# Log-sum-exp over rows: the first load as eight transfers of every eighth partition instead of two transfers of all partitions

## The chip, the cores and the metric

The kernel runs on one core of a Trainium2 chip. The metric is the device time of one execution in microseconds (us); the runs of the kernel before took 161.5 us in the median of three (161.47 to 161.6).

## The reference

```python
x = np.random.randn(32, 512, 1024).astype(np.float32)

def reference(x):
    max_x = np.max(x, axis=-1, keepdims=True)
    return (max_x.squeeze(-1) + np.log(np.sum(np.exp(x - max_x), axis=-1))).astype(np.float32)
```

The input has 16,384 rows of 1,024 numbers, 67.11 MB. One number comes out per row.

## The kernel before

The rows are laid over 128 partitions. Each partition owns 128 rows of 1,024 float32 (4 KB each): 112 that lie one behind another in memory, and 16 of a second block. The kernel takes the exponential without subtracting the maximum, sums it and takes the logarithm; a small side calculation finds out whether any sum left the range in which this is safe, and only then a second, slower branch is run. With this input it is not.

The input comes in 18 loads (table `LOADS`), from 16 rows per partition at the start down to half a row at the end. All go into `ring`, a buffer of 48 rows per partition, so three loads of 16 rows fit without waiting. For each load, in this order:

- SP (SyncE) issues the transfer in `load()`, after a wait for whoever still used that part of the ring. The transfer adds 16 to the semaphore `landed[i]` when it is complete.
- ScalarE (ACT in the profile) waits for `landed[i]` and takes the exponential in place (line 235).
- VectorE (DVE) sums each row, by `reduce_sum` (line 246, "R"), or after GpSimd (POOL, line 240) has added the two halves of each row ("F", summed in line 177), or with a fused add of the halves (line 256, "T").

So SP's issue of load 3 waits for VectorE's sum of load 0, which had its place in the ring, and so on round the ring. The last row goes in two pieces through line 209. Two stores write the logarithms; the first waits for the last load but one.

Load 0 is special in two ways. It is issued as two transfers: first `FIRST` = 512 elements of each partition (half a row, 2 KB), then the other 15.5 rows. ScalarE waits for both, with `landed[0]` at 16 for each transfer. And both issues are moved to the head of the program by `start_early`, ahead of the barrier with which all engines begin; `first_loads` holds them. Behind that barrier stand ScalarE's load of the function table (line 127), VectorE's memsets of constants (lines 128 to 131), and SP's issues of all other loads.

A load with all 128 partitions has 128 runs of memory, one per partition. A run is one packet of the profile: 64 KB for a load of 16 rows, 2 KB and 62 KB for the two parts of load 0. Sixteen packets are under way at a time.

Of the kernel before, what the change touches and what calls it, by code (L numbers as in the profile page):

```python
# [16 lines left out]
B = 16  # L17
LATE = 119
AHEAD = 1
FIRST = 512  # L20

# [31 lines left out]
def kernel(  # L55
# [5 lines left out]
    nc = tc.nc  # L61
# [4 lines left out]
    P = nc.NUM_PARTITIONS  # L66
# [19 lines left out]
    def source(e0, size):  # L86
        assert e0 >= W * d or e0 + size <= W * d
        return x_rest[:, e0 - W * d : e0 - W * d + size] if e0 >= W * d else x_rows[:, e0 : e0 + size]
# [8 lines left out]
    def sbuf(name, cols, dtype=fp32, rows=P):  # L97
        return nc.alloc_sbuf_tensor(name, [rows, cols], dtype).ap()

    ring = sbuf("ring", RING * d)  # L100
# [15 lines left out]
    landed = [nc.alloc_semaphore(f"landed{i}") for i in range(len(loads))]  # L116
# [19 lines left out]
    def load(i, here, done_before, size):  # L136
        for a, b, who, at in users:
            if a < here + size and b > here:
                sp.wait(who, at)
        users[:] = [u for u in users if not (u[0] < here + size and u[1] > here)]  # L140
        parts = [(0, FIRST), (FIRST, size)] if i == 0 else [(0, size)]
        return [
            nc.sync.dma_start(
                out=ring[:, here + a : here + b], in_=source(done_before + a, b - a)
            ).then_inc(landed[i], 16)
            for a, b in parts
        ]

    def check_early():
# [36 lines left out]
    here = 0  # L186
    early_sum = 0
    done_before = 0
# [3 lines left out]
    for i, (size, ops) in enumerate(loads):  # L192
# [3 lines left out]
        if any(q < here + size and q + t * d > here for _, t, q, _ in folded):  # L196
            reduce_folded()
        dma = load(i, here, done_before, size)
        if i < AHEAD:
            first_loads.extend(x.ins for x in dma)  # L200
# [3 lines left out]
        for k, (how, s) in enumerate(ops):  # L204
            rows = ring[:, p : p + s * d].rearrange("p (c d) -> p c d", d=d)
            if how in "YZ":
# [3 lines left out]
                    out=last_exp[:, here - p : end - p], in_=ring[:, here:end], func=AF.Exp,  # L210
# [4 lines left out]
                here = end  # L215
# [5 lines left out]
            elif how == "A":  # L221
# [3 lines left out]
                    out=v, in_=v, func=AF.Exp, accum_out=sumexp[:, c : c + 1]  # L225
# [5 lines left out]
            else:  # L231
# [4 lines left out]
                here = upto  # L236
            if how == "F":
# [3 lines left out]
                    out=rows[:, :, 0:H], in0=rows[:, :, 0:H], in1=rows[:, :, H:d], op=ALU.add  # L241
                ))
                folded.append((c, s, p, at))
            elif how == "R":
                dve.wait(act, at)
                who = (dve, dve.did(nc.vector.reduce_sum(  # L246
                    out=sumexp[:, c : c + s], in_=rows, axis=AX.X
                )))
                users.append((p, p + s * d, *who))
            elif how == "T":  # L250
# [3 lines left out]
                for r in range(s):  # L254
                    lo = rows[:, r, 0:H]
                    who = (dve, dve.did(nc.vector.scalar_tensor_tensor(  # L256
                        out=lo, in0=lo, scalar=1.0, in1=rows[:, r, H:d],
# [13 lines left out]
            if c == LATE:  # L271
# [4 lines left out]
                    out=res[:, 0:W], in_=sumexp[:, 0:W], func=AF.Ln  # L276
# [14 lines left out]
        out=res[:, LAST:NC], in_=last_sum, func=AF.Ln, bias=sumexp[:, LAST:NC]  # L291
# [8 lines left out]
        out=clamped[:, LATE:NC], in0=sumexp[:, LATE:NC], scalar=LOW,  # L300
# [10 lines left out]
        out=over[:, 0:half], in0=last_piece[:, 0:half], scalar=CEILING,  # L311
# [16 lines left out]
    with nc.If(all_fine < 1):  # L328
# [5 lines left out]
        for c0 in range(0, NC, RING):  # L334
# [6 lines left out]
            for c1, c2 in ((c0, edge), (edge, c0 + s)):  # L341
                if c1 == c2:
                    continue
                nc.scalar.dma_start(
                    out=ring[:, (c1 - c0) * d : (c2 - c0) * d],
                    in_=source(c1 * d, (c2 - c1) * d),
# [4 lines left out]
                out=neg, in_=v, op=ALU.max, axis=AX.X, negate=True  # L351
# [3 lines left out]
                out=v, in0=v, in1=neg[:, :, None].to_broadcast([P, s, d])  # L355
# [5 lines left out]
                out=sumexp[:, c0 : c0 + s], in_=v, axis=AX.X  # L361
# [71 lines left out]
```

## Time and profile before

| | |
|---|---|
| time, median of 3 runs | 161.5 us |
| the profiled execution's own time | 161.57 us |
| its span in the profile | 160.2 us |
| ACT busy | 114.5 us (71% of the span) |
| DVE busy | 114.3 us (71%) |
| POOL busy | 37.3 us (23%) |
| PE busy | 2.2 us (1%) |
| read from the chip's memory | 67.11 MB |

The span starts with SP's first issue. The page lists busy times by engine, and the span in 40 slices of 4.0 us. "SPq" is SP's queue of transfer issues; its rows tell how long the issue takes, not the transfer. A row of the timeline reads: start, length, engine, line, operation, output and input with shapes, how many instructions were merged; in brackets how long the engine was idle before, and what ended that.

### The profile page before, as it was taken

What the parts mean: (1) busy time and instruction counts of PE and PEld (TensorE: products, weight loads), DVE (VectorE), ACT (ScalarE), POOL (GpSimd) and SP (SyncE); (2) the same over time, 40 slices, a digit from 0 to 9 for tenths busy, and PEclk for the clock granted to TensorE, in tenths of its full rate; (3) what the DMA queues carried; (4) which work ended last, traced back from release to release, by engine and by line L of the source; (5) the groups of instructions that cost most, each with busy time, mean ns of one, the idle gap of its engine ahead of it and who ended that gap; (6) DMA issues with size and microseconds to landing.
All of it is one profiled execution on the core that took longest, in us unless ns stands there. A gap on an engine that the chain in (4) does not pass through costs nothing.

```text
span 160.2 us, 221 instructions
## 1 busy us (share of the span) xinstructions
PE 2.2 (1%) x26; PEld 1.1 (1%) x26; DVE 114.3 (71%) x59; ACT 114.5 (71%) x31; POOL 37.3 (23%) x11
## 2 busy tenths in 40 slices
PE   0000000000000000000000000000000000000022
PEld 0000000000000000000000000000000000000011
DVE  0000000009999499994999859959999999999996
ACT  3000059980799708995099949992999989799996
POOL 0000000000000000000000994690004969891000
DMA  9996996996996996997999999999999999999992
GB/s 319 507 460 301 507 524 262 524 524 262 524 524 262 524 524 262 524 474 311 483 442 442 442 425 409 409 409 471 423 414 417 458 409 399 444 412 428 415 408 97
DMA packets 3025, 67.18 MB, mean 419 GB/s; under 512 B 592, under 2 KB 720, under 8 KB 1488
## 3 DMA queue, kind: packets, MB, share of 16 engines
q1 hardware_dynamic: 3024, 67.18, 97.8%
q14 instruction: 1, 0.01, 0.0%
HBM read 67.11 MB, written 0.07 MB: 419 GB/s over the span
## 4 chain that ended last, share of the span: by engine, by line
DMA 51%; ACT 28%; DVE 19%; issue 1%; PE 0%
DMA ring<-in_x_dram 51%; ACT ring L235 28%; DVE sumexp L246 16%; DVE sumexp L177 2%; DVE ring L256 1%; DVE over L310 0%; PE count L315 0%; ACT res L275 0%; DVE clamped L299 0%; DVE fine L317 0%; DVE sumexp L219 0%
## 5 line engine op out<-in xcount | busy, mean ns | idle before, releaser
L235 ACT ACTIVATE ring<-ring 128x16384 f32<-128x16384 f32 (+16 forms) x23 | 111.7, 4908 | 42.3 <-DMA ring<-in_x_dram 42.3
L246 DVE TENSOR_REDUCE sumexp<-ring 128x16 f32<-128x16384 f32 (+4 forms) x9 | 85.6, 9513 | 42.1 <-ACT ring L235 42.1
L240 POOL TENSOR_TENSOR ring<-ring 128x3072 f32<-128x3072 f32 (+3 forms) x7 | 37.1, 5315 | 107.2 <-ACT ring L235 107.2
L177 DVE TENSOR_REDUCE sumexp<-ring 128x6 f32<-128x3072 f32 (+3 forms) x7 | 18.4, 2659 | 0.0
L256 DVE SCALAR_TENSOR_TENSOR ring<-ring 128x512 f32<-128x512 f32 x15 | 9.6, 687 | 0.4 <-ACT ring L235 0.4
L127 ACT ACT_TABLE_LOAD x1 | 1.3, 1283 | 1.9 <-PEq L64 1.9
L162 PE MATMUL count<-far,bad 128*1 128x1 f32 x2 | 0.2, 164 | 153.0 <-DVE clamped L157 153.0
L166 PE MATMUL count<-sumexp,ones 128*1 128x1 f32 x18 | 1.6, 164 | 3.6 <-DVE ring L256 3.6
L128 DVE MEMSET ones<- 128x1 f32 x1 | 0.1, 59 | 2.0 <-PEq L64 2.0
L256 DVE DVE_READ_ACCUMULATOR ring<-ring 128x1 f32 x15 | 1.2, 82 | 0.0
L209 ACT ACTIVATE last_exp<-ring 128x544 f32<-128x544 f32 (+1 forms) x2 | 1.2, 588 | 0.0
L162 PEld LDWEIGHTS count<-far,bad 128*1 128x1 f32 x2 | 0.1, 82 | 153.0 <-DVE clamped L157 153.0
L166 PEld LDWEIGHTS count<-sumexp,ones 128*1 128x1 f32 x18 | 0.8, 81 | 4.4 <-DVE ring L256 4.4
L310 DVE SCALAR_TENSOR_TENSOR over<-ring 128x240 f32<-128x240 f32 x1 | 0.4, 404 | 0.0
L317 DVE TENSOR_SCALAR fine<-count 1x1 int32<-1x1 f32 x1 | 0.1, 147 | 0.3 <-PE count L315 0.3
L157 DVE SCALAR_TENSOR_TENSOR clamped<-clamped,sumexp 128x119 f32<-128x119 f32 x1 | 0.3, 283 | 0.0
L275 ACT ACTIVATE res<-sumexp 128x112 f32<-128x112 f32 x1 | 0.3, 279 | 0.0
L290 ACT ACTIVATE res<-last_sum,sumexp 128x1 f32<-128x1 f32 x1 | 0.3, 261 | 0.0
L209 ACT ACTIVATION_READ_ACCUMULATOR last_exp<-ring 128x1 f32 x2 | 0.3, 129 | 0.0
L152 DVE TENSOR_SCALAR clamped<-sumexp 128x119 f32<-128x119 f32 x1 | 0.2, 222 | 0.0
L288 ACT ACTIVATE res<-sumexp 128x15 f32<-128x15 f32 x1 | 0.2, 213 | 0.0
L299 DVE SCALAR_TENSOR_TENSOR clamped<-sumexp 128x9 f32<-128x9 f32 x1 | 0.2, 170 | 0.0
(17 smaller groups left out, 1.8 us busy)
## 6 DMA issues: line engine op xcount, KB each, us to landing
ring<-in_x_dram SPq DMA_DIRECT2D x1, 7936.0 KB, 21.3
ring<-in_x_dram SPq DMA_DIRECT2D x1, 6912.0 KB, 23.9
ring<-in_x_dram SPq DMA_DIRECT2D x1, 6400.0 KB, 19.7
ring<-in_x_dram SPq DMA_DIRECT2D x1, 4608.0 KB, 15.9
ring<-in_x_dram SPq DMA_DIRECT2D x1, 3584.0 KB, 24.0
ring<-in_x_dram SPq DMA_DIRECT2D x1, 3072.0 KB, 19.1
ring<-in_x_dram SPq DMA_DIRECT2D x1, 2288.0 KB, 24.2
ring<-in_x_dram SPq DMA_DIRECT2D x1, 1664.0 KB, 20.9
```

Source lines behind the costliest of these rows:

```text
L127: nc.scalar.preload_act_table_set("natural_log_exp_and_others")
L157: dve.did(nc.vector.scalar_tensor_tensor(out=clamped[:, 0:LATE], in0=clamped[:, 0:LATE], scalar=0.0, in1=sumexp[:, 0:LATE], op0=ALU.bypass ...
L162: pe.did(nc.tensor.matmul(count, lhsT=bad[:, 0:1], rhs=far, start=True, stop=False))
L166: return pe.did(nc.tensor.matmul(count, lhsT=ones, rhs=sumexp[:, c : c + 1], **kw))
L177: at = dve.did(nc.vector.reduce_sum(out=sumexp[:, c0 : c0 + s0], in_=halves, axis=AX.X))
L209: at = act.did(nc.scalar.activation(out=last_exp[:, here - p : end - p], in_=ring[:, here:end], func=AF.Exp, accum_out=first_sum if how == ...
L235: at = act.did(nc.scalar.activation(out=v, in_=v, func=AF.Exp))
L240: at = pool.did(nc.gpsimd.tensor_tensor(out=rows[:, :, 0:H], in0=rows[:, :, 0:H], in1=rows[:, :, H:d], op=ALU.add))
L246: who = (dve, dve.did(nc.vector.reduce_sum(out=sumexp[:, c : c + s], in_=rows, axis=AX.X)))
L256: who = (dve, dve.did(nc.vector.scalar_tensor_tensor(out=lo, in0=lo, scalar=1.0, in1=rows[:, r, H:d], op0=ALU.mult, op1=ALU.add, accum_out ...
L275: ln_early = act.did(nc.scalar.activation(out=res[:, 0:W], in_=sumexp[:, 0:W], func=AF.Ln))
L310: dve.did(nc.vector.scalar_tensor_tensor(out=over[:, 0:half], in0=last_piece[:, 0:half], scalar=CEILING, in1=last_piece[:, half : 2 * half ...
```

## The change

Load 0 is issued as eight transfers instead of two. Transfer k, of 0 to 7, has the partitions k, k+8, ..., k+120, 16 of them, and all 16 rows of each: 16 runs of 64 KB. All eight add to the same semaphore, and ScalarE waits for 8 x 16 = 128. All eight go ahead of the opening barrier. The other loads are as they were, one transfer of 128 partitions each.

```diff
-FIRST = 512
+GROUP = 8
...
-        parts = [(0, FIRST), (FIRST, size)] if i == 0 else [(0, size)]
+        to, what = ring[:, here : here + size], source(done_before, size)
+        step = GROUP if i == 0 else 1
         return [
-            nc.sync.dma_start(
-                out=ring[:, here + a : here + b], in_=source(done_before + a, b - a)
-            ).then_inc(landed[i], 16)
-            for a, b in parts
+            nc.sync.dma_start(out=to[k:P:step], in_=what[k:P:step]).then_inc(landed[i], 16)
+            for k in range(step)
         ]
```

On SP, at the head of the program, there stood before (`in_x_dram` is the input; the branch in row 2 leaves the opening barrier; "dve" is VectorE's counter of finished instructions):

```order
0 L143 DMA ring<-in_x_dram 128x512
1 L143 DMA ring<-in_x_dram 128x15872
2 L428 UNCONDITIONAL_BRANCH [waits barrier_Pool_Activation_PE_DVE_SP_release]
3 L143 DMA ring<-in_x_dram 128x16384 [waits barrier_Pool_Activation_PE_DVE_SP_release]
4 L143 DMA ring<-in_x_dram 128x16384
5 L143 DMA ring<-in_x_dram 128x16384 [waits dve]
6 L143 DMA ring<-in_x_dram 128x13824 [waits dve]
```

And now:

```order
0 L144 DMA ring<-in_x_dram 16x16384 x8
1 L427 UNCONDITIONAL_BRANCH [waits barrier_Pool_Activation_PE_DVE_SP_release]
2 L144 DMA ring<-in_x_dram 128x16384 [waits barrier_Pool_Activation_PE_DVE_SP_release]
3 L144 DMA ring<-in_x_dram 128x16384
4 L144 DMA ring<-in_x_dram 128x16384 [waits dve]
5 L144 DMA ring<-in_x_dram 128x13824 [waits dve]
```

The two issues at the head became eight; behind them, the barrier and the other loads stand in the same order with the same waits. On ScalarE, what stands behind the barrier is the same before and after, but for the line numbers:

```order
0 L427 UNCONDITIONAL_BRANCH [waits barrier_Pool_Activation_PE_DVE_SP_release]
1 L127 ACT_TABLE_LOAD [waits barrier_Pool_Activation_PE_DVE_SP_release]
2 L234 ACTIVATE ring<-ring 128x16384 [waits landed0]
3 L234 ACTIVATE ring<-ring 128x16384 [waits landed1]
4 L234 ACTIVATE ring<-ring 128x16384 [waits landed2]
```

The first exponential waits for `landed0`, which now counts eight transfers.

## The prediction

> **What bounds the kernel now.** I read the page's slices and DMA part first, then the chain of waits, then the timeline of the first 60 us. The page, parts 2 and 3:
>
> ```profile
> DMA  9996996996996996997999999999999999999992
> GB/s 319 507 460 301 507 524 262 524 524 262 524 524 262 524 524 262 524 474 311 483 442 442 442 425 409 409 409 471 423 414 417 458 409 399 444 412 428 415 408 97
> ...
> q1 hardware_dynamic: 3024, 67.18, 97.8%
> HBM read 67.11 MB, written 0.07 MB: 419 GB/s over the span
> ```
>
> The one load queue is busy for 97.8% of the span. The sixes, and the 262 beside 524, are no gaps: a packet of 64 KB is booked in the slice in which it starts, so a slice gets one or two rounds of 16 packets (1.05 MB each). The chain of waits, in order of time (start, length, what):
>
> ```profile
> 1.92 39.19 DMA ring<-in_x_dram
> ...
> 41.13 13.87 ACT ring L235
> ...
> 55.02 17.23 DVE sumexp L246
> ...
> 72.27 23.91 DMA ring<-in_x_dram
> ...
> 118.95 19.09 DMA ring<-in_x_dram
> 138.04 0.02 issue
> 138.06 12.36 ACT ring L235 x5
> ```
>
> The chain is loads until 138.06 us, and from there ScalarE, which then never waits for a load again. The piece at 72.27 looks like a stall on the ring but is not: that transfer needs 23.91 us because others lie ahead of it. The timeline shows this:
>
> ```profile
> 21.79 13.86 ACT L235 ACTIVATE ring<-ring 128x16384 f32<-128x16384 f32 x1 [18.58 <-DMA ring<-in_x_dram]
> 35.67 17.22 DVE L246 TENSOR_REDUCE sumexp<-ring 128x16 f32<-128x16384 f32 x1 [33.54 <-ACT ring L235]
> 41.13 13.86 ACT L235 ACTIVATE ring<-ring 128x16384 f32<-128x16384 f32 x1 [5.49 <-DMA ring<-in_x_dram]
> ...
> 60.49 13.86 ACT L235 ACTIVATE ring<-ring 128x16384 f32<-128x16384 f32 x1 [5.51 <-DMA ring<-in_x_dram]
> ```
>
> Loads 0, 1 and 2 land just before 21.79, 41.13 and 60.49. Load 1 takes 19.34 us behind load 0, load 2 takes 19.36: for 128 rows of 64 KB (8.39 MB) that is 434 GB/s, 27.1 GB/s for each of 16 streams, 2.42 us for a packet of 64 KB. Each exponential is over 5.5 us before the next load lands. So the kernel is one stream of loads; whatever moves the landing of load 0 moves everything behind it.
>
> Now the start, as windows (window, length, busy of PE, PEld, DVE, ACT, POOL, clock, DMA share, GB/s):
>
> ```profile
> 0.00:1.00 1.00, 0.00 (x0) 0.00 (x0) 0.00 (x0) 0.00 (x0) 0.20 (x4) 1.00 0.00 0
> 1.00:2.00 1.00, 0.00 (x0) 0.00 (x0) 0.01 (x1) 0.08 (x1) 0.00 (x0) 1.00 0.92 211
> ...
> 21.40:41.00 19.60, 0.00 (x0) 0.00 (x0) 5.33 (x1) 13.86 (x1) 0.00 (x0) 1.00 1.00 435
> 41.00:60.00 19.00, 0.00 (x0) 0.00 (x0) 16.88 (x2) 13.86 (x1) 0.00 (x0) 1.00 0.98 424
> ```
>
> No packet moves before 1.0 us. Load 0 is there at 21.79, and 1.0 + 19.35 is 20.35: 1.44 us go to the first bytes' way and the landing, part of it to the half row in 2 KB packets, which runs at 211 GB/s.
>
> **The change part by part.** *SP's issues.* From the timeline of SP's queue, each row from its own window:
>
> ```profile
> 0.00 0.39 SPq L143 DMA_DIRECT2D ring<-in_x_dram  x1
> ...
> 0.44 0.42 SPq L143 DMA_DIRECT2D ring<-in_x_dram  x1
> ...
> 1.92 0.86 SPq L143 DMA_DIRECT2D ring<-in_x_dram  x2
> ...
> 52.92 0.33 SPq L143 DMA_DIRECT2D ring<-in_x_dram  x1
> ```
>
> Two issues become eight ahead of the barrier. Back to back they start 0.44 to 0.48 us apart (0.00, 0.44; the pair at 1.92 takes 0.86), so the six added cost 6 x 0.45 = 2.7 us of SP. Behind them on SP stand the barrier and the issues of loads 1 and 2, which go from 1.92 to about 4.6; nobody misses those before load 0 is through, 20 us at the least. Behind the barrier wait the other engines: ScalarE's table load and VectorE's four memsets.
>
> ```profile
> 1.92 1.28 ACT L127 ACT_TABLE_LOAD   x1 [1.92 <-PEq L64]
> 1.99 0.06 DVE L128 MEMSET ones<- 128x1 f32 x1 [1.99 <-PEq L64]
> ```
>
> They go 2.7 us later, under the 18.58 us that ScalarE idles before 21.79. Cost nothing; with that cover gone, 2.7 us. One issue in the program took much longer than the rest:
>
> ```profile
> L143 SPq DMA_DIRECT2D ring<-in_x_dram x19: 327/424/1543, 0.0 to 136.8; - x19
> ```
>
> If it was a full queue (it stands at 136.8, with several small loads still out), load 2's issue may meet the same limit now, with nine transfers out before it. It has until load 1 is through, so this costs nothing either.
>
> *The half row goes.* Of the 1.44 us, the 2 KB packets have a share: 262 KB at 434 GB/s is 0.6 us, and at the 211 of the window 1.2. So 0.6 us at most is saved; the first large packets will be slow to start as well, so I take 0.4, between 0 and 0.6. The semaphore steps of eight transfers instead of two hardly count: the boundary between loads 1 and 2 is inside the 19.36, equal to the 19.34 before to 0.02 us.
>
> *Which rows are under way together.* This is the term that decides. Before, a transfer has 128 rows, eight for each of 16 streams. Now each has 16 rows, one for each stream, 64 KB long, and the 16 are partitions k, k+8, ..., k+120. All streams work through k = 0 to 7 in the same order, so the rows under way are always (nearly) those of one k. What one packet costs then, the trace of before does not show: all its loads have 128 partitions. The lower end is the row of load 1, 2.42 us a packet, 19.35 for the load. For the upper end, ask what the 434 GB/s is. It is the same in 21.4 to 41 us (435) with ScalarE at 13.86 us busy, and in 41 to 60 (424, a whole number of packets off) with VectorE on top at 16.88, so the compute engines don't set it. It is a fixed rate of 27.1 GB/s, sixteen times. If that belongs to the streams, nothing changes. If it belongs to sixteen ways into the on-chip memory, each for eight partitions, it matters which eight. Sixteen ways take four of the seven bits of a partition's number; the rows of one k differ in the bits of 8, 16, 32 and 64 only. Where one of the bits of 1, 2 and 4 takes part in the choice and one of those four does not, the 16 rows reach eight ways, two packets in each, and the other eight ways are empty: 4.84 us a packet, 8 x 4.84 = 38.7 for the load, 19.35 more. I take this upper end. The chosen rows vary only half of what can tell partitions apart, and full rate needs the choice to be by exactly the four bits that vary: blocks of eight neighbours. Both ends stay for the range.
>
> [...]
>
> *Sum.* Load 0 lands 19.35 - 0.4 = 18.95 us later, near 40.7. What follows is a plain shift. Loads 1 and 2 are queued, their rows spread over all partitions again, and they run at 19.35 each. Load 3 is issued when VectorE has reduced load 0 (35.67 + 17.22 = 52.89, the issue at 52.92); that moves to 71.9. The stream runs dry only when load 2 is through (60.5, moving to 79.4), so the 7.5 us of cover stay. From load 3 on all releases and landings are shifted alike, the last wait at 138.06 and the 22 us behind it too. The profiled execution took 161.57 us for its span of 160.2: 161.57 + 18.95 = 180.5. It stands 0.07 above the median of the runs, so against that the forecast is **180.4 us**.
>
> Range of this case: 0 to 0.6 for the half row gives 180.3 to 180.9. The factor 2 may be off by some per cent, 5% of 38.7 being 1.9 us; hence 178 to 183.
>
> **The rivals.**
>
> *No sharing: faster.* The 27.1 GB/s belong to the streams, or each way serves eight neighbours. For it: the packet of the nearest row, load 1, has the same 64 KB and takes 2.42 us. Against it: those packets run beside others than the change puts together. Load 0 then gains the 0 to 0.6 of the half row: 161.5 - 0.4 = 161.1, from 160.9 to 161.5. It decides if load 0 lands by 21.8 us. What a measurement of this kernel can tell from no change is 0.2%, 0.32 us, so about two thirds of this case are "faster".
>
> *Rows bound to streams.* A partition may always be served by the same stream, also in a transfer of 16 rows. Then the rows of k = 0 to 3 sit on eight streams, two on each, and those of 4 to 7 on the other eight. Both halves work at once, eight packets each, but the second half starts with the fifth issue: 4 x 0.45 = 1.8 us late. Load 0 lands 1.8 - 0.4 = 1.4 later: 162.9. For it: nothing in the trace says how rows are dealt out. Against it: that needs a deal by partition number rather than by the row's place in the transfer. [...]
>
> *Uneven sharing.* Two packets share a way, but one goes first. Then one stream of each pair is through k = 0 to 3 after 4 x 2.42 = 9.7 us and goes on into the empty ways, while the other starts on k = 0 to 3: load 0 ends 9.7 us late instead of 19.35, 161.5 + 9.7 - 0.4 = 170.8. Anything between this and the forecast is possible. Against it: the streams in the trace keep step, since whole loads take 19.34 and 19.36.
>
> **How the numbers follow.** Even sharing, 180.4: 0.81. It is a judgement on how partitions are told apart, which no row decides; that a load of every eighth partition is spread as well as one of all of them needs one particular choice. No sharing, 161.1: 0.12, split 0.08 faster and 0.04 within 0.2%. Rows bound to streams, 162.9: 0.04. Uneven sharing, 170.8 and up: 0.03. Slower by over 0.2% is thus 0.88, the same 0.04, faster 0.08. The range 178 to 183 holds the first case but for a sliver; the others, 0.19, lie outside it.
>
> **What would show it.** Right: ScalarE's first exponential on the ring starts near 40.7 us instead of 21.79, with an idle time near 35 before it; the windows up to 40 us show about 217 GB/s, and from then 434; loads 1 and 2 land 19.35 apart as before; the exponential of line 235 (now 234) has the same lengths; SP's pair of issues for loads 1 and 2 starts near 4.6, or the second of them is drawn out; the end follows the last wait by the same 22 us; the span is near 179.1. A first exponential at 21.3 is the first rival, at 23.2 the second, near 31 the third. The forecast is wrong if packets of load 0 take 2.4 us each, and wrong in its size if a gap stands between the eight transfers, or if the stream runs dry after load 2 because load 3 was late by more than 7.5 us.

## The result and the profile after

The changed kernel takes 183.05 us (median of four runs, 182.97 to 183.07) against 161.5 before: a ratio of 1.1332, with a 95% interval of 1.1313 to 1.1352. It is slower, and 0.05 us beyond the upper end of the predicted range.

The timeline of the changed kernel, with the rows that answer to those shown of before:

```profile
43.38 13.86 ACT L234 ACTIVATE ring<-ring 128x16384 f32<-128x16384 f32 x1 [35.79 <-DMA ring<-in_x_dram]
57.27 17.22 DVE L245 TENSOR_REDUCE sumexp<-ring 128x16 f32<-128x16384 f32 x1 [50.75 <-ACT ring L234]
62.57 13.86 ACT L234 ACTIVATE ring<-ring 128x16384 f32<-128x16384 f32 x1 [5.33 <-DMA ring<-in_x_dram]
74.52 0.33 SPq L144 DMA_DIRECT2D ring<-in_x_dram  x1
```

The first exponential starts at 43.38 us instead of 21.79, 21.59 later; the second 21.44 later. The span grew from 160.2 to 181.7, by 21.5. So all of the loss is in load 0, and what follows is the old schedule moved as a whole: the compute instructions have their old lengths, load 3 is issued when VectorE has reduced load 0, with load 2 still under way.

The page's rate row (slices of 4.5 us), and two windows of the changed kernel (window, length, busy of PE, PEld, DVE, ACT, POOL, clock, DMA share, GB/s):

```profile
GB/s 231 231 231 231 231 216 144 115 216 462 447 317 390 462 462 462 462 462 447 361 346 462 414 560 390 375 519 383 369 495 406 427 410 442 412 427 410 432 404 130
```

```profile
0.00:41.00 41.00, 0.00 (x0) 0.00 (x0) 0.15 (x4) 1.28 (x1) 0.20 (x4) 1.00 0.99 205
41.20:60.50 19.30, 0.00 (x0) 0.00 (x0) 3.23 (x1) 13.86 (x1) 0.00 (x0) 1.00 1.03 435
```

The streams are busy all the time (0.99) and move less than half: 205 GB/s until load 0 is through, 435 right after it. A packet's mean time can be read from such a row. The first window holds the 128 packets of load 0 and nothing else (205 GB/s x 41 us = 8.4 MB), eight to a stream, so a packet takes 0.99 x 41 / 8 = 5.07 us in the mean (5.05 to 5.10, since the share is rounded). Before, by the same reading of load 1, it is 1.01 x 19.1 / 8 = 2.41:

```profile
20.90:40.00 19.10, 0.00 (x0) 0.00 (x0) 4.33 (x1) 13.86 (x1) 0.00 (x0) 1.00 1.01 439
```

### The profile page after: what moved, and what is told of

Its sections match the earlier page's. It is cut to its first block, busy times and chain, and to the rows that moved or that the text cites. A ratio compares the mean times of both kernels' runs of the same rounds, so it can differ in the third digit from the quotient of the medians.

```text
span 181.7 us, 227 instructions
## 1 busy us (share of the span) xinstructions
PE 2.2 (1%) x26; PEld 1.1 (1%) x26; DVE 114.3 (63%) x59; ACT 114.5 (63%) x31; POOL 37.3 (21%) x11
## 4 chain that ended last, share of the span: by engine, by line
DMA 45%; ACT 32%; DVE 16%; another core or an unknown queue 3%; SPq 2%; issue 1%; PE 0%
DMA ring<-in_x_dram 45%; ACT ring L234 32%; DVE sumexp L245 14%; SPq L144 2%; DVE sumexp L176 2%; DVE ring L255 0%; DVE over L309 0%; PE count L314 0%; ACT res L274 0%; DVE clamped L298 0%; DVE fine L316 0%; DVE sumexp L218 0%
## 6 DMA issues: line engine op xcount, KB each, us to landing
ring<-in_x_dram SPq DMA_DIRECT2D x1, 3072.0 KB, 19.1
```

## The experiments

Each changes only how a load is cut into transfers. `to` and `what` are load 0's place in the ring and its source, with partitions first and columns second. A "way" is, as in the prediction, one of sixteen paths into the on-chip memory: the author's estimate from sixteen streams at 27.1 GB/s, which no run shows as such.

**Near sources.** The same partitions are written, from source rows side by side.

```diff
-dma_start(out=to[k:P:8], in_=what[k:P:8])
+dma_start(out=to[k:P:8], in_=what[16 * k : 16 * k + 16])
```

> As the change, but transfer k fills partitions k, k+8, ..., k+120 from 16 source rows that lie side by side (16k to 16k+15), so the first 16 results of each partition come out at other places. Ways into the on-chip memory (my theory): the partitions written together are the same as in the change, so the time is that of the change, 183 us, first exponential near 43.4 us. Memory side (rival: the sixteen source rows 3.67 MB apart collide in the chip's memory): the sources are now 0.46 MB apart, so load 0 runs at full rate: 161 to 162 us, first exponential near 22.

Measured, in one run: 183.52 us. Its first exponential:

```profile
43.81 13.86 ACT L235 ACTIVATE ring<-ring 128x16384 f32<-128x16384 f32 x1 [36.22 <-DMA ring<-in_x_dram]
```

43.81 against 43.38 in the change: near sources bring none of the 21.59 us back. The cause is in which partitions are written together.

**Neighbours.** Both sides in blocks of 16 neighbouring partitions.

```diff
-dma_start(out=to[k:P:8], in_=what[k:P:8])
+dma_start(out=to[16 * k : 16 * k + 16], in_=what[16 * k : 16 * k + 16])
```

> Eight transfers of sixteen neighbouring partitions (16k to 16k+15), source and destination. [...] Memory side: full rate, 161 to 162 us. Each way for eight neighbours: two ways, 2.42 x 8 = 19.3 a packet, 155 for the load, 297 us.

Measured, in one run: 215.71 us. The first exponential, and windows of this kernel, the first holding the packets of load 0 alone:

```profile
76.06 13.86 ACT L235 ACTIVATE ring<-ring 128x16384 f32<-128x16384 f32 x1 [69.90 <-DMA ring<-in_x_dram]
```

```profile
0.00:71.00 71.00, 0.00 (x0) 0.00 (x0) 0.15 (x4) 1.28 (x1) 0.20 (x4) 1.00 1.02 118
73.00:92.00 19.00, 0.00 (x0) 0.00 (x0) 2.05 (x1) 13.86 (x1) 0.00 (x0) 1.00 1.01 424
```

A packet takes 1.02 x 71 / 8 = 9.05 us, 3.7 times the 2.42: near a quarter of the rate, 118 GB/s against the 424 right after. The memory side and blocks of eight neighbours (161 and 297 us) are both out. This run and the one with near sources read the same source rows in the same order and differ only in the partitions written, and load 0 lands at 76.06 instead of 43.81.

The packet takes 7% less than four times the 2.42 here, where in the change it takes 5% more than twice. Why one lies below its multiple and the other above, no run shows, and the two can't be set beside each other as prices, since the streams don't keep step here: of the sixteen packets of the second round, six begin in the window below (328 GB/s x 1.20 us = 6 x 64 KB) and the other ten outside it. In the changed kernel all sixteen of the fourth round begin within 1.50 us (699 GB/s x 1.50 us = 16 x 64 KB), and so do those of the fifth; a packet takes about 5.1 us (3.42 x 1.50) in the fourth and 4.95 (3.30 x 1.50) in the fifth. The window of the neighbours, then the fourth and fifth rounds of the changed kernel:

```profile
8.50:9.70 1.20, 0.00 (x0) 0.00 (x0) 0.00 (x0) 0.00 (x0) 0.00 (x0) 1.00 2.87 328
```

```profile
15.90:17.40 1.50, 0.00 (x0) 0.00 (x0) 0.00 (x0) 0.00 (x0) 0.00 (x0) 1.00 3.42 699
...
21.00:22.50 1.50, 0.00 (x0) 0.00 (x0) 0.00 (x0) 0.00 (x0) 0.00 (x0) 1.00 3.30 699
```

**One transfer.** Load 0 undivided, without the half row.

```diff
-dma_start(out=to[k:P:8], in_=what[k:P:8])   # k = 0 to 7
+dma_start(out=to, in_=what)
```

> Load 0 as one transfer of 128 partitions with 16 rows, ahead of the barrier: the change without the division by partitions. My theory: the half row in small packets was worth 0.0 to 0.6 us of loss, so 160.9 to 161.5 us. Rival (the half row brings the first bytes sooner and its removal costs): 161.6 to 162.0; then 0.4 us or less of the 21.5 us loss of the change are due to it.

Measured: 161.61 us, ratio 1.0003 [0.9994, 1.0012]. Its first exponential:

```profile
21.81 13.86 ACT L235 ACTIVATE ring<-ring 128x16384 f32<-128x16384 f32 x1 [19.08 <-DMA ring<-in_x_dram]
```

21.81 against 21.79: the half row is worth nothing either way. The 0.4 us that the sum credited for its removal are not there.

**Eight of all partitions.** Eight transfers by columns instead of by partitions; `d` is the 1,024 elements of a row.

```diff
-dma_start(out=to[k:P:8], in_=what[k:P:8])
+dma_start(out=to[:, 2 * d * k : 2 * d * (k + 1)], in_=what[:, 2 * d * k : 2 * d * (k + 1)])
```

> Load 0 as eight transfers of two rows each of all 128 partitions, all ahead of the barrier: eight issues, eight times sixteen landings and the late barrier as in the change, but every transfer reaches all partitions. My theory: issues, landings and the barrier's delay cost nothing, 161.0 to 161.6 us, packets of 8 KB at the rate of the others. Rival (eight transfers cost in themselves, by gaps or by the late barrier): 163 us and more, up to 183 if the division by rows had nothing to do with it.

Measured: 162.0 us, ratio 1.0029 [1.0017, 1.0041], slower than expected by 0.4 us. From the timeline of this kernel:

```profile
5.10 1.28 ACT L127 ACT_TABLE_LOAD   x1 [5.10 <-PEq L64]
22.21 13.86 ACT L235 ACTIVATE ring<-ring 128x16384 f32<-128x16384 f32 x1 [15.83 <-DMA ring<-in_x_dram]
```

The barrier is late, if less so than in the change (ScalarE's table load at 5.10 us, in the change 6.31, before 1.92), and ScalarE still waits 15.83 us for load 0. That load comes 0.42 us later, with 64 packets to a stream instead of 16; that this is about 9 ns for each of the 48 is argued from the count alone. Eight issues and a late barrier thus cost at most 0.4 us here, against the 21.5 of the change.

**Every fourth partition.** Four transfers of 32 rows.

```diff
-dma_start(out=to[k:P:8], in_=what[k:P:8])   # k = 0 to 7
+dma_start(out=to[k:P:4], in_=what[k:P:4])   # k = 0 to 3
```

> [...] Rows dealt by their place in the transfer (streams take rows two by two, or row s and s+16): at any time two packets stand at each of eight ways, packets near 5.09 us, time near 183 us as in the change. Rows dealt by partition (each stream keeps one way): packets of 2.42 us and 161.5 to 162.2 us, the issues 0.58 us apart costing nothing.

Measured: 162.16 us, ratio 1.0036 [1.002, 1.0052]. The window of this kernel that holds load 0's packets (8.4 MB):

```profile
0.00:20.50 20.50, 0.00 (x0) 0.00 (x0) 0.15 (x4) 1.28 (x1) 0.20 (x4) 1.00 0.98 409
```

A packet takes 0.98 x 20.5 / 8 = 2.51 us: near the 2.42 of load 1, and with a first round of 3.04, as in the run with one transfer, (3.04 + 7 x 2.42) / 8 = 2.50 is the estimate for the full rate. Rows far apart are no harm as such, nor is a transfer of a part of the partitions. Of the two times expected the second came in, the one for rows dealt by partition; how they are dealt is argued from this rate, since no row tells which stream took which row.

**Half runs.** Sixteen transfers, the columns in two halves.

```diff
-dma_start(out=to[k:P:8], in_=what[k:P:8])
+dma_start(out=to[k:P:8, half], in_=what[k:P:8, half])   # left halves for k = 0 to 7, then right
```

> The change with runs of 32 KB: sixteen transfers of every eighth partition, first the left half of the columns, then the right. It asks what the 5.09 us of a packet are beyond 2 x 2.42 = 4.84. A lower rate of a way that two streams share: packets of 2.55 us, load 0 as late as in the change, 183 us. A cost of each packet (0.25 us): packets of 2.67 us, load 0 some 2 us later than in the change, 185 us.

Measured: 182.58 us. Again the window with load 0's packets, here sixteen to a stream:

```profile
0.00:40.70 40.70, 0.00 (x0) 0.00 (x0) 0.15 (x4) 1.28 (x1) 0.20 (x4) 1.00 0.99 206
```

A packet of 32 KB takes 0.99 x 40.7 / 16 = 2.52 us, half of 5.07. What lies above the double is a rate, not a cost of each packet, which would have given 2.67.

**Four apart and two apart.** Sixteen rows at other distances.

```diff
-dma_start(out=to[k:P:8], in_=what[k:P:8])
+dma_start(out=to[64 * g + k : 64 * g + 64 : 4], ...)   # g = 0, 1; k = 0 to 3
```

> Eight transfers of 16 rows four partitions apart: 0, 4, ..., 60 first, then 1 to 61 and so on, then the upper 64. The rows differ in the bits of 4, 8, 16 and 32. [...]

```diff
-dma_start(out=to[k:P:8], in_=what[k:P:8])
+dma_start(out=to[32 * g + k : 32 * g + 32 : 2], ...)   # g = 0 to 3; k = 0, 1
```

> Eight transfers of 16 rows two partitions apart: 0, 2, ..., 30 first. The rows differ in the bits of 2, 4, 8 and 16. [...]

Measured: 182.81 us and 183.18 us. The windows of load 0's packets, first with rows four apart, then with rows two apart:

```profile
0.00:41.00 41.00, 0.00 (x0) 0.00 (x0) 0.15 (x4) 1.28 (x1) 0.20 (x4) 1.00 0.98 205
```

```profile
0.00:41.00 41.00, 0.00 (x0) 0.00 (x0) 0.15 (x4) 1.28 (x1) 0.20 (x4) 1.00 0.99 205
```

5.02 and 5.07 us a packet. In the change and in these two, the sixteen rows of a transfer lie eight, four and two partitions apart, and the price is nearly the same: 5.07, 5.02 and 5.07 us, 4 to 5% beyond the double of 2.42.

**The second load.** The kernel before, with load 1 cut instead of load 0.

```diff
-dma_start(out=to, in_=what)                 # load 1
+dma_start(out=to[k:P:8], in_=what[k:P:8])   # k = 0 to 7, load 1; load 0 as before
```

> The kernel before, with load 1 (not load 0) as eight transfers of every eighth partition: load 0 keeps its half row, its two transfers and its early issue, so nothing of the start is changed. If the loss of the change is 21.1 us of shared ways (8 packets of 5.05 instead of 2.42 us) and 0.4 of a longer first issue: 161.5 + 21.1 = 182.6 us, load 1 landing 40.4 us behind load 0. If the packets cost the double alone and the other 2 us are a matter of the start: 161.5 + 19.35 = 180.9 us.

Measured: 182.96 us, ratio 1.1325 [1.1306, 1.1344]. From the timeline, the exponentials of loads 0 and 1:

```profile
22.00 13.86 ACT L237 ACTIVATE ring<-ring 128x16384 f32<-128x16384 f32 x1 [18.80 <-DMA ring<-in_x_dram]
...
62.41 13.86 ACT L237 ACTIVATE ring<-ring 128x16384 f32<-128x16384 f32 x1 [26.55 <-DMA ring<-in_x_dram]
```

Load 1 lands 62.41 - 22.00 = 40.41 us behind load 0, where before it was 19.34: 21.07 us for rows eight apart with nothing of the start in it. So of the 21.59 us in the change almost all is the rate, and about 0.5 is left for the start. Load 0 itself came 0.21 us later than before, for which no row names a cause.

No version beats the kernel before; undivided load 0 equals it.

## Why the prediction went as it did

**Right: the bound and the shift.** One stream of loads set the time. The last wait for a load moved from 138.06 to 159.49, and 22.2 us follow it (22.1 before). From the chain of waits of the changed kernel:

```profile
159.49 12.34 ACT ring L234 x5
```

Load 3's issue had its cover: it came at 74.52, and load 2, still under way, is through about 7 us later (62.57 + 19.35 = 81.9).

**Right: which rows are under way together.** This term decided, as the prediction had it, and the end it took was the right one: 5.07 us a packet is near 4.84 and far from 2.42. Near sources (43.81 against 43.38) exclude the memory side; what counts is the partitions written together. The patterns give, a packet: 2.51 us for 32 rows four apart, 5.02 to 5.07 for sixteen rows eight, four or two apart, 9.05 for sixteen neighbours, against 2.42 for all partitions. That the rows of one k share eight ways, two to each, was the author's estimate: it fits the factor of the change, but no run shows how many ways there are or which partitions share one. From the rows of before the prediction could not know the factor; it called the choice "a judgement on how partitions are told apart, which no row decides". The rivals are out: no sharing and uneven sharing by the packet's 5.07 us, rows bound to streams by a landing at 43.4 instead of 23.2.

**Wrong: three sizes in one sum.** "Load 0 lands 19.35 - 0.4 = 18.95 us later" was short by 2.6 us.

- The packet, put at the double, 4.84 us, for two streams in one way, takes 5.07: 8 x 0.23 = 1.8 us, the largest part. The run with load 1 cut gives the same without the start: 21.07 us instead of 19.35, 1.7 more.
- The half row's 0.4 us: none, by the run with one transfer. The 1.2 us at 211 GB/s was read as loss that its removal saves. But without the half row the sixteen large packets of the first round take 3.04 us each (share 3.04 over 1.00 us), not 2.42. The prediction had said "the first large packets will be slow to start as well", and still credited the 0.4. In the changed kernel the first round is not slow, at 4.90 us; there the time beside first bytes and packets is 43.38 - 1.35 - 40.6 = 1.4 us, where the sum had left 1.44 - 0.4 = 1.0. Where in the changed kernel that time goes stays open. The window with the first round of large packets, one transfer first, then the change:

```profile
1.00:2.00 1.00, 0.00 (x0) 0.00 (x0) 0.15 (x4) 0.55 (x1) 0.00 (x0) 1.00 3.04 1049
```

```profile
1.00:2.00 1.00, 0.00 (x0) 0.00 (x0) 0.00 (x0) 0.00 (x0) 0.00 (x0) 1.00 4.90 1049
```

- The first bytes: the prediction left their start where it was, at 1.0 us, with "the six added cost 6 x 0.45". The first issue with a step of eight between partitions took 0.58 us, against 0.39 without one before. SP's queue in the changed kernel, from windows of their own, and the windows at the first bytes, changed kernel first, then before:

```profile
0.00 0.58 SPq L144 DMA_DIRECT2D ring<-in_x_dram  x1
...
0.00 5.00 SPq L144 DMA_DIRECT2D ring<-in_x_dram  x8
...
6.30 0.82 SPq L144 DMA_DIRECT2D ring<-in_x_dram  x2
```

```profile
1.00:1.35 0.35, 0.00 (x0) 0.00 (x0) 0.00 (x0) 0.00 (x0) 0.00 (x0) 1.00 0.00 0
```

```profile
1.00:1.35 0.35, 0.00 (x0) 0.00 (x0) 0.00 (x0) 0.00 (x0) 0.00 (x0) 1.00 1.30 123
```

Up to 1.35 us no byte moves where before packets ran: at least 0.35 us. That the step makes the issues longer, and not the sixteen rows, the run with neighbours shows: its ten issues up to load 2, eight of them of sixteen rows too, take 5.70 us, against 7.12 in the change. The three terms make 1.8 + 0.4 + 0.35 = 2.55 of the 2.6.

The range had room for two of the three. Its upper end was 180.9, with nothing for the half row, plus 1.9, "5% of 38.7", for the factor 2: 182.8, written as 183. Both came out near these bad ends. The first bytes had no term in the sum, and their 0.35 us are more than the 0.2 between 182.8 and 183.

**Right for the wrong size: the issues cost nothing.** Eight take 5.00 us, and loads 1 and 2 go out at 6.30, not 4.6; ScalarE's table load moved by 4.4 us, not 2.7. All of it lay under the wait for load 0, 35.79 us now. The pair at 6.30 takes 0.82 (0.86 before), so neither was drawn out.

## What to carry to other kernels

Where loads set the time, look at which partitions are written at the same moment: here a packet of 64 KB took 5.02 to 5.07 us with sixteen rows at a step of 8, 4 or 2, where it took 2.42 in a load of all partitions, 9.05 with sixteen neighbours, and 2.51 with 32 rows at a step of 4. In the profile of this case the mark of it is a busy share of 0.99 beside 205 GB/s, where the next load shows 435. When a sum rests on a factor that no row has shown, the range needs its spread together with the small terms at their bad ends, and room for what the sum puts at nothing. Here each came out near its bad end, and first bytes 0.35 us later, for which there was no term, were enough to leave the range.

## What the runs showed of the hardware

- A stream moves 64 KB in 2.42 us in a load of all partitions (27.1 GB/s), and in 5.07 us when the sixteen rows under way are eight partitions apart (12.9 GB/s). That this is more than the double was not expected, and why it is so stays open; it is a rate, since runs of 32 KB take half, 2.52 us. The 9.05 us of the run with neighbours can't be set beside it as a price, since its streams don't keep step (six of sixteen packets of the second round begin within 1.20 us).
- The first issue of a transfer whose partitions are eight apart takes SP 0.58 us, against 0.39 for one of all partitions (the half row of before), and its first bytes come at least 0.35 us later, more than the 0.19 by which the issue is longer.
- Transfers of 32 rows at a step of 4 come near the full rate, 2.51 us a packet against 2.42, so a transfer need not span every partition for that.
